# Compressed keys and values in a hybrid decoder block: the first product with the weights stationary

## The chip, the cores and the metric

The kernel runs on one core of a Trainium2 chip. The metric is the device time of one execution in microseconds (us). All arithmetic is float32; where a product runs on TensorE as float32r, each operand is split into a rounded high part and a low part (the rest), and the product is made of up to three products of parts.

## The reference

A decoder block over 256 tokens with 2048 features: one wide input projection, a gated short convolution beside sparse attention with 16 query heads and 4 key and value heads, a residual layer norm, an MLP and per-layer embeddings. What matters here is the compression of the keys and of the values, cut from the reference:

```python
def _compress(k, pe, w1, w2):
    B, T, Hk, Dh = k.shape                       # 1, 256, 4, 128
    n_cmp = (T - CMP_LEN) // CMP_STRIDE + 1      # 15 blocks of 32 tokens, 16 apart
    idx = jnp.arange(n_cmp)[:, None] * CMP_STRIDE + jnp.arange(CMP_LEN)[None, :]
    blocks = k[:, idx] + pe[None, None, :, None, :]
    blocks = jnp.moveaxis(blocks, 3, 2).reshape(B, n_cmp, Hk, CMP_LEN * Dh)
    return jax.nn.gelu(blocks @ w1) @ w2         # w1: 4096 x 256, w2: 256 x 128
```

Four heads with 15 blocks each are 60 rows; the first product has 4096 features to sum over, in 32 slices of 128, and 256 hidden features as its result.

## The kernel before

The weights stream from memory in pieces of 512 KB at most. A piece is loaded by SyncE's queue into one of four buffers (`raw`, L74), ScalarE writes its rounded high part (`whi`, L68, four buffers), VectorE the low part (`wlo`, L69, three buffers), and TensorE uses both. The big projections have two forms. `wstat` (L98, L104) takes 256 columns of the weights as stationary operand: per slice of 128 features two products of 512 moving columns (both parts of the tokens) and two of 256. `xstat` (L124, L125, L128) takes the tokens as stationary operand and moves 512 or 280 columns of weights.

The order of the work is written out by generators. `weave` runs a main generator and a side generator, with the side's steps spread evenly over the main's. Here the main one has 40 steps, four `wstat` of four steps each (keys of the two other branches) and three `xstat` of eight; the side one is `compress` for the keys and then for the values, 24 steps. The order of TensorE's instructions in the trace differs a little from that of the program: a product whose low part isn't ready yet stands behind later work.

`compress` first lays out the 60 blocks by position (`blk`, both parts, L263 to the split). Then, for each of the 32 positions `l`, it multiplies: the blocks' two parts, 120 columns side by side, are the stationary operand, and the 256 hidden features of the weights' high part (L273) and of their low part (L274) move. The result `ph` has the blocks on partitions, in one PSUM bank (tag `po`). ScalarE copies it out (L277), two transposes (L281) bring the features onto partitions in another bank (tag `tp`), and VectorE adds the two halves (L286, L287) and computes the gelu with ScalarE's tanh (L288 to L293). The second product follows a step later: for the keys L298 (float32, 60 moving columns), for the values L317 (float32, 64 stationary and 128 moving columns), both in the bank `po`.

Of the kernel before, what the change touches and what calls it, by code (L numbers as in the profile page):

```python
# [10 lines left out]
F32 = mybir.dt.float32  # L11
# [5 lines left out]
P = 128  # L17
# [8 lines left out]
HID = 2 * HD  # L26
# [6 lines left out]
GELU_C = 0.7978845608028654  # L33
# First distances of the log-spaced buckets 16, 17, ... (distances below 16 have one bucket each).
LOG_STARTS = (16, 23, 32, 46, 64, 91, 128, 182)

# Column offsets of w_in.
C_BG, C_CG, C_HX, C_Q = 0, D, 2 * D, 3 * D
# [7 lines left out]
def block_kernel(ctx: ExitStack, tc: tile.TileContext, x, p, w_in, conv_w, cmp_pe_k, cmp_w1_k, cmp_w2_k,  # L46
# [24 lines left out]
    def load_raw(src, nk, n):  # L71
        """A [nk*128, n] piece of a weight matrix, rows on partitions."""
        raw = wp.tile([P, nk, n], F32, tag="raw", name="raw", bufs=4)
        nc.sync.dma_start(raw, src.rearrange("(k p) n -> p k n", p=P))  # L74
        return raw

    def wchunk(src, nk, n):
        """The same as two float32r parts."""
        raw = load_raw(src, nk, n)
        hi = wp.tile([P, nk, n], F32R, tag="whi", name="whi", bufs=4)  # L80
        lo = wp.tile([P, nk, n], F32R, tag="wlo", name="wlo", bufs=3)
        split(raw, hi, lo)
        return hi, lo

    def wstat(src, c0, mov, evac, r0=0, nk=4, ahead=None):
        """256 columns of src as the stationary operand, both parts of mov side by side as the moving one.
        evac(f, A, B): features f*128 .. of the result are A + B, [feature, token] each."""
        ps = [ps_mm.tile([P, 2, T], F32, tag="mm", name="mm") for _ in range(2)]
        for k0 in range(0, KT, nk):
            hi, lo = wchunk(src[r0 + k0 * P:r0 + (k0 + nk) * P, c0:c0 + 256], nk, 256)  # L90
            for kk in range(nk):
                kt = k0 + kk
                if ahead is not None:
                    ahead(kt)

                def high():
                    for f in range(2):
                        nc.tensor.matmul(ps[f].rearrange("p a t -> p (a t)"), hi[:, kk, f * P:(f + 1) * P],  # L98
                                         mov[:, kt].rearrange("p a t -> p (a t)"), start=(kt == 0),
                                         stop=(kt == KT - 1), skip_group_check=True)  # L100

                def low():
                    for f in range(2):
                        nc.tensor.matmul(ps[f][:, 1, :], lo[:, kk, f * P:(f + 1) * P], mov[:, kt, 0, :],  # L104
                                         start=False, stop=False, skip_group_check=True)

                for part in ((high, low) if kt < KT - 1 else (low, high)):
                    part()
            yield
        for f in range(2):  # L110
            evac(f, ps[f][:, 0, :], ps[f][:, 1, :])

    def xstat(src, c0, n, sta, evac, r0=0, nkt=KT, ahead=None):
        """n columns of src as the moving operand, sta as the stationary one: evac(t, [token, n])."""
        ps = [ps_mm.tile([P, n], F32, tag="mm", name="mm") for _ in range(NT)]
# [26 lines left out]
    def weave(main, n_main, side, n_side):  # L142
        """Steps of side spread evenly over the steps of main."""
        done = 0
# [5 lines left out]

# [1 line left out]
    ident = const.tile([P, P], F32, name="ident")  # L152
    make_identity(nc, ident)
    NV = (3 + 2) * KT
    vecT = const.tile([P, NV], F32, name="vecT")  # conv taps, then ln1 gain and offset, features on partitions
    gate = const.tile([P, NT, 3 * NH], F32, name="gate")
# [9 lines left out]
    def transposed(nat, kt):  # L166
        """Columns kt*128 .. of two 128-token tiles, features on partitions."""
        pool, tag = turns[kt // 2 % len(turns)]
# [19 lines left out]

    # In these the two float32r parts are the dimension before the last, or before the branch in the keys.
    att = ctx.enter_context(ExitStack())  # L190
# [9 lines left out]
    with tc.tile_pool(name="front", bufs=1) as fp:  # L200
# [19 lines left out]

        # Taps, gains and offsets by feature; bias by distance, -127 up to 255.
        vecs = fp.tile([NV, P], F32, name="vecs")
# [21 lines left out]

# [1 line left out]
        nb = NKV * NCMP  # L246
        blk = big.tile([P, 2, CMP_LEN, 2, NKV * NCMP], F32R, tag="B", name="blk")

        def compress(i, pe, w1, w2):
# [16 lines left out]
            yield  # L266
            ph = ps_po.tile([2 * nb, HID], F32, tag="po", name="ph")
            for l4 in range(CMP_LEN // 4):
                hi, lo = wchunk(w1[0][l4 * 512:(l4 + 1) * 512, :], 4, HID)
                for k in range(4):  # L270
                    l = 4 * l4 + k
                    b = blk[:, i, l].rearrange("p a n -> p (a n)")
                    nc.tensor.matmul(ph, b, hi[:, k, :], start=(l == 0), stop=False)  # L273
                    nc.tensor.matmul(ph, b, lo[:, k, :], start=False, stop=(l == CMP_LEN - 1))  # L274
                yield
            hs = fp.tile([2 * nb, HID], F32, tag="hs", name="hs")
            nc.scalar.activation(hs, ph, AF.Copy)  # L277
            yield
            tp = ps_tp.tile([P, 2, 2, 64], F32, tag="tp", name="tp")
            for e in range(2):  # L280
                nc.tensor.transpose(tp[:, e].rearrange("p a n -> p (a n)")[:, :2 * nb],  # L281
                                    hs[:, e * P:(e + 1) * P], ident[:2 * nb, :2 * nb])
            both = tp.rearrange("p e a n -> p e (a n)")
            g0 = fp.tile([P, 2, nb], F32, tag="g0", name="g0")
# [19 lines left out]
            else:  # L304
                # A row of vrep for each of a group's four heads and 16 blocks, the last of which is zero.
                hx = ap.tile([P, 2, NKV, 4, 16], F32, tag="s1", name="hx")
# [15 lines left out]
        def v_window(lo_cols):  # L322
            # The window's values and the gates' logits are 560 columns side by side.
            def evac(t, ps):
# [7 lines left out]
        def keys(i, h):  # L332
# [5 lines left out]
        weave(chain(*proj), 40, chain(compress(0, cmp_pe_k, cmp_w1_k, cmp_w2_k),  # L338
                                      compress(1, cmp_pe_v, cmp_w1_v, cmp_w2_v)), 24)

# [1 line left out]
    o = big.tile([P, NH, T], F32, tag="O", name="o")  # L342
# [8 lines left out]
    def conv_block(cp, c):  # L351
        """Channels c*128 .. c*128 + 255."""
        cg = cp.tile([P, 2, T], F32, tag="cg", name="cg")
# [22 lines left out]

    # Products of two split operands: parts of the one and of the other.
    parts = ((0, 0), (1, 0), (0, 1))
# [4 lines left out]
    def attend(j, q):  # L383
        """Heads 4j .. 4j + 3, of key and value head j."""
        # bias[q, g, i] is at distance q + i - 127, so that key k of the first w keys is at i = w - 1 - k.
        bias = ap.tile([P, 4, T], F32, tag="bias", name="bias", bufs=1)
# [5 lines left out]
        nc.vector.tensor_copy(cb[:, 1, :, 0:15], back(bias, 224, (T, 4), (-16, 15)))  # L392
        # The compressed keys as columns (g, c) for head g, zero elsewhere.
        nc.vector.tensor_copy(back(kcp, 0, (4 * 64, 2), (64 + 16, 4), (1, 16)),
# [66 lines left out]
        def values(pair, pT):  # L461
            """Two heads' outputs, [feature, query tile, head, query]."""
            # Row (g, c) of the compressed values for head g, zero elsewhere.
            vm = ap.tile([64, 2, 2, HD], F32R, tag="vm", name="vm", bufs=1)
# [25 lines left out]
        for g in range(4):  # L490
# [3 lines left out]
            if g % 2 == 0:  # L494
                # Of each part and branch the blocks (keys 0, queries 0), (0, 1), (1, 1) of two heads.
                pT = ap.tile([P, 2, 2, 3, 2, P], F32R, tag="pT", name="pT", bufs=1)
# [18 lines left out]

# [1 line left out]
    post = ctx.enter_context(tc.tile_pool(name="post", bufs=2))  # L517
# [30 lines left out]

# [1 line left out]
    xres = big.tile([P, NT, D], F32, tag="O", name="xres")  # L550
# [31 lines left out]

# [1 line left out]
    x1 = big.tile([P, KT, 2, T], F32R, tag="X", name="x1")  # L584
# [51 lines left out]

# [1 line left out]
    stats2 = post.tile([P, NT, 4, 6], F32, tag="st", name="stats2", bufs=1)  # L638
# [48 lines left out]

    # The last columns with all their weights at hand, so that the first tokens are done early.
    wh = big.tile([P, KT, 512], F32R, tag="X", name="wh")
# [21 lines left out]
def _onehot():  # L711
    """Bucket of each distance -127 .. 255, a column each; the last row stands for what is masked."""
    e = np.zeros((NB + 1, 384), np.float32)
# [45 lines left out]
```

## Time and profile before

| | |
|---|---|
| median of 3 runs | 1865.37 us (1864.33 to 1865.76) |
| span of the profiled execution | 1864.0 us |
| TensorE matmul, busy | 1839.1 us (99%) |
| TensorE weight load, busy | 1577.8 us (85%) |
| VectorE, busy | 1157.9 us (62%) |
| ScalarE, busy | 879.3 us (47%) |

The profile gives the profiled execution by its span, from its first instruction to its last; the median of the runs is 1.37 us above it. Durations of matmuls overlap, since they are pipelined and their ends are modelled, so the distance from one start to the next says more of the pace than a duration does. PE stands for matmuls and PEld for weight loads of TensorE, DVE for VectorE, ACT for ScalarE, SP for SyncE.

### The profile page before, as it was taken

The page shows a single profiled execution, that of the slowest core. Times are in us where ns is not written, and L with a number is a line of the kernel's source. Part 1 is how long each engine was busy: PE and PEld are TensorE (multiplying, and loading weights), DVE is VectorE, ACT ScalarE, POOL GpSimd, SP SyncE. Part 2 cuts the span into 40 slices and gives each one's busy share as a digit, 9 for nine tenths or more (in the row PEclk, how much of TensorE's full clock was granted, in tenths as well). Part 3 has the DMA queues.
Part 4 walks back from the last instruction along what each step waited for, and adds up shares of the span by engine and source line. Part 5 has one row for each costly group of instructions (what it writes and reads, how often), then busy time and mean ns, then how long its engine had stood idle before and what let it go on. Part 6 is the DMA issues. An engine that isn't in the chain of part 4 may idle for free.

```text
span 1864.0 us, 25953 instructions
## 1 busy us (share of the span) xinstructions
PE 1839.1 (99%) x9921; PEld 1577.8 (85%) x9921; DVE 1157.9 (62%) x1668; ACT 879.3 (47%) x1269; POOL 43.2 (2%) x42
## 2 busy tenths in 40 slices
PE   8999999999999999999999899999999999999997
PEld 7889888888888888888888688888888888888886
DVE  6676776767677555565555865655565556556664
ACT  5555554545556444444443444443444344434541
POOL 1000000000000000000000500000000000000001
PEclk9999999999999999999999999999999999999998
DMA  8767565555555766666665466655665566556671
GB/s 249 231 201 240 171 170 164 164 169 170 160 165 171 220 188 187 192 192 183 191 236 193 169 204 192 191 191 188 196 187 191 193 189 190 192 192 192 193 243 72
DMA packets 295068, 352.98 MB, mean 189 GB/s; under 512 B 11125, under 2 KB 240853, under 8 KB 294176
## 3 DMA queue, kind: packets, MB, share of 16 engines
q1 hardware_dynamic: 291328, 342.27, 59.5%
q10 hardware_dynamic: 3232, 8.65, 1.3%
q8 instruction: 77, 1.26, 0.3%
q0 software_dynamic: 384, 0.41, 0.1%
q14 instruction: 47, 0.39, 0.1%
HBM read 349.17 MB, written 2.12 MB: 188 GB/s over the span
## 4 chain that ended last, share of the span: by engine, by line
PE 96%; DVE 2%; DMA 1%; issue 0%; ACT 0%; SPq 0%; POOLq 0%; POOL 0%; DVEq 0%
PE mm L98 42%; PE mm L104 21%; PE mm L125 9%; PE mm L124 9%; PE mm L128 9%; PE mm L705 1%; PE pss L436 1%; DVE x L69 1%; PE po L473 1%; DMA raw<-in_w_mlp_down_dram 1%; PE tp L458 1%; DVE wlo L69 0%; PE ph L274 0%; PE ph L273 0%; PE po L482 0%; PE po L477 0%
## 5 line engine op out<-in xcount | busy, mean ns | idle before, releaser
L69 DVE TENSOR_TENSOR wlo<-raw,whi 128x1024 fp32r<-128x1024 f32 (+2 forms) x648 | 781.6, 1209 | 596.7 <-PE mm L104 298.6
L68 ACT ACTIVATE whi<-raw 128x1024 fp32r<-128x1024 f32 (+2 forms) x648 | 676.8, 1046 | 683.3 <-PE mm L98 314.6
L98 PE MATMUL mm<-xT,whi 128*128 128x512 f32 x1792 | 562.7, 397 | 0.0
L104 PEld LDWEIGHTS mm<-xT,wlo 128*128 128x128 f32 x1792 | 328.6, 188 | 73.3 <-issue 0.2
L104 PE MATMUL mm<-xT,wlo 128*128 128x256 f32 x1792 | 349.0, 280 | 0.0
L98 PE MATMUL mm<-x,whi 128*128 128x512 f32 x1024 | 316.8, 395 | 0.0
L98 PEld LDWEIGHTS mm<-xT,whi 128*128 128x128 f32 x1792 | 279.3, 189 | 6.0 <-issue 0.6
L104 PEld LDWEIGHTS mm<-x,wlo 128*128 128x128 f32 x1024 | 187.9, 188 | 42.5
L104 PE MATMUL mm<-x,wlo 128*128 128x256 f32 x1024 | 196.7, 279 | 0.0
L125 PE MATMUL mm<-whi,h 128*128 128x512 f32 x480 | 186.8, 389 | 0.0
L124 PE MATMUL mm<-whi,h 128*128 128x512 f32 x480 | 186.7, 389 | 0.0
L98 PEld LDWEIGHTS mm<-x,whi 128*128 128x128 f32 x1024 | 158.4, 189 | 2.8
L128 PE MATMUL mm<-wlo,h 128*128 128x512 f32 x480 | 147.9, 389 | 0.6 <-DVE wlo L69 0.6
L128 PEld LDWEIGHTS mm<-wlo,h 128*128 128x128 f32 x480 | 90.0, 188 | 19.6 <-DVE wlo L69 1.0
L125 PEld LDWEIGHTS mm<-whi,h 128*128 128x128 f32 x480 | 90.1, 188 | 18.8
L124 PEld LDWEIGHTS mm<-whi,h 128*128 128x128 f32 x480 | 90.1, 188 | 18.7
L98 PE MATMUL mm<-aT,whi 128*128 128x512 f32 x256 | 80.4, 395 | 0.0
L98 PE MATMUL mm<-oT,whi 128*128 128x512 f32 x256 | 80.3, 395 | 0.0
L104 PEld LDWEIGHTS mm<-oT,wlo 128*128 128x128 f32 x256 | 47.0, 188 | 10.6
L104 PEld LDWEIGHTS mm<-aT,wlo 128*128 128x128 f32 x256 | 46.9, 188 | 10.5
L125 PE MATMUL mm<-whi,x 128*128 128x512 f32 x128 | 50.2, 404 | 2.8 <-DVE x L69 2.8
L125 PE MATMUL mm<-whi,mix 128*128 128x512 f32 x128 | 49.8, 389 | 0.0
(210 smaller groups left out, 1636.5 us busy)
## 6 DMA issues: line engine op xcount, KB each, us to landing
raw<-in_w_in_dram SPq DMA_DIRECT2D x228, 512.0 KB, 3.7
raw<-in_w_mlp_up_dram SPq DMA_DIRECT2D x128, 512.0 KB, 3.8
raw<-in_w_mlp_down_dram SPq DMA_DIRECT2D x128, 512.0 KB, 3.8
raw<-in_w_conv_out_dram SPq DMA_DIRECT2D x32, 512.0 KB, 3.4
raw<-in_w_attn_out_dram SPq DMA_DIRECT2D x32, 512.0 KB, 3.4
raw<-in_w_mix_out_dram SPq DMA_DIRECT2D x32, 512.0 KB, 4.0
raw<-in_w_ple_gate_dram SPq DMA_DIRECT2D x32, 512.0 KB, 4.1
raw<-in_w_in_dram SPq DMA_DIRECT2D x16, 280.0 KB, 3.4
```

The lines of the kernel that those rows point to most:

```text
L68: nc.scalar.activation(hi, src, AF.Copy)
L69: nc.vector.tensor_sub(lo, src, f32(hi))
L98: nc.tensor.matmul(ps[f].rearrange("p a t -> p (a t)"), hi[:, kk, f * P:(f + 1) * P], mov[:, kt].rearrange("p a t -> p (a t)"), start=(kt ...
L104: nc.tensor.matmul(ps[f][:, 1, :], lo[:, kk, f * P:(f + 1) * P], mov[:, kt, 0, :], start=False, stop=False, skip_group_check=True)
L124: nc.tensor.matmul(ps[t], sta[:, kt, 0, ts], hi[:, kk, :], start=(kt == 0), stop=False)
L125: nc.tensor.matmul(ps[t], sta[:, kt, 1, ts], hi[:, kk, :], start=False, stop=False)
L128: nc.tensor.matmul(ps[t], sta[:, kt, 0, ts], lo[:, kk, :], start=False, stop=(kt == nkt - 1))
L436: nc.tensor.matmul(ps, q[:, g, a, t * P:(t + 1) * P], kT[:, j, b, :, :w], start=(n == 0), stop=(n == 2))
L458: nc.tensor.transpose(tp[:, b, k, :], s[:, b, k * P:(k + 1) * P], ident)
L473: nc.tensor.matmul(po, vn[:, b, 0, a, vs], pT[:, c, b, 0:2], start=(n == 0 and b == 0), stop=False, skip_group_check=True)
L705: nc.tensor.matmul(ps, h[:, kt, a, ts], w[:, kt, :], start=(kt == 0 and n == 0), stop=(kt == KT - 1 and n == 2))
```

## The change

The first product of `compress` changes its form. For each position the weights' 128x128 pieces are now the stationary operand, two halves `e` of the hidden features with a high and a low part each. The blocks move: both parts (120 columns) over a high piece, the high part alone (60 columns) over a low piece, added to the columns of the blocks' low part. So there are four products a position in place of two, and the product of the two low parts is left out. The result `ph` has the features on partitions, so the copy by ScalarE and the two transposes go, with one step, and VectorE reads `ph` itself. Keys and values together have 22 side steps in place of 24. The other lines of the diff are comments, which are left out here.

```diff
-            ph = ps_po.tile([2 * nb, HID], F32, tag="po", name="ph")
+            ph = ps_po.tile([P, 2, 2 * nb], F32, tag="po", name="ph")
             for l4 in range(CMP_LEN // 4):
                 hi, lo = wchunk(w1[0][l4 * 512:(l4 + 1) * 512, :], 4, HID)
                 for k in range(4):
                     l = 4 * l4 + k
                     b = blk[:, i, l].rearrange("p a n -> p (a n)")
-                    nc.tensor.matmul(ph, b, hi[:, k, :], start=(l == 0), stop=False)
-                    nc.tensor.matmul(ph, b, lo[:, k, :], start=False, stop=(l == CMP_LEN - 1))
+                    for e in range(2):
+                        es = slice(e * P, (e + 1) * P)
+                        nc.tensor.matmul(ph[:, e, :], hi[:, k, es], b, start=(l == 0 and e == 0), stop=False,
+                                         skip_group_check=True)
+                        nc.tensor.matmul(ph[:, e, nb:], lo[:, k, es], b[:, :nb], start=False,
+                                         stop=(l == CMP_LEN - 1 and e == 1), skip_group_check=True)
                 yield
-            hs = fp.tile([2 * nb, HID], F32, tag="hs", name="hs")
-            nc.scalar.activation(hs, ph, AF.Copy)
-            yield
-            tp = ps_tp.tile([P, 2, 2, 64], F32, tag="tp", name="tp")
-            for e in range(2):
-                nc.tensor.transpose(tp[:, e].rearrange("p a n -> p (a n)")[:, :2 * nb],
-                                    hs[:, e * P:(e + 1) * P], ident[:2 * nb, :2 * nb])
-            both = tp.rearrange("p e a n -> p e (a n)")
+            both = ph
...
-                                      compress(1, cmp_pe_v, cmp_w1_v, cmp_w2_v)), 24)
+                                      compress(1, cmp_pe_v, cmp_w1_v, cmp_w2_v)), 22)
```

## Rows read from the trace of the kernel before

**Rows 1.** The page's busy shares: busy us, share of the span and instructions, TensorE's matmuls and weight loads.

```profile
PE 1839.1 (99%) x9921; PEld 1577.8 (85%) x9921; DVE 1157.9 (62%) x1668; ACT 879.3 (47%) x1269; POOL 43.2 (2%) x42
```

**Rows 2.** The page's chain of work that ended last, share of the span by engine.

```profile
PE 96%; DVE 2%; DMA 1%; issue 0%; ACT 0%; SPq 0%; POOLq 0%; POOL 0%; DVEq 0%
```

**Rows 3.** Busy time of each engine in the two windows that hold the compression: window and its length, then PE, PEld, DVE, ACT and POOL busy us with instructions, granted TensorE clock as a share of 2.4 GHz, DMA share, GB/s.

```profile
36.00:120.00 84.00, 84.00 (x492) 73.78 (x491) 55.55 (x68) 45.78 (x60) 0.00 (x0) 1.00 0.74 226
120.00:175.00 55.00, 53.86 (x359) 49.18 (x358) 38.63 (x53) 31.08 (x43) 0.74 (x1) 1.00 0.73 218
```

**Rows 4.** Matmuls of the compression grouped by line and shape, from 36 to 600 us: line, engine, operation, output and inputs, stationary operand (partitions * columns), moving operand (partitions x columns), count | busy us, mean ns of one | idle us before.

```profile
L273 PE MATMUL ph<-whi,blk 128*120 128x256 f32 x64 | 16.4, 283 | 0.6 <-DVE blk L69 0.6
L274 PE MATMUL ph<-wlo,blk 128*120 128x256 f32 x64 | 15.9, 282 | 0.0
L281 PE MATMUL tp<-ident,hs 120*128 120x120 f32 x4 | 0.7, 265 | 0.0
```

**Rows 5.** One step of the first product in the timeline (start us, duration us): its first matmul, its last, and the next operation's.

```profile
76.37 0.28 PE L273 MATMUL ph<-whi,blk 128*120 128x256 f32 x1
...
77.19 0.28 PE L274 MATMUL ph<-wlo,blk 128*120 128x256 f32 x1
...
77.30 0.62 PE L98 MATMUL mm<-xT,whi 128*128 128x512 f32 x2
```

**Rows 6.** Weight loads grouped by line and shape, from 36 to 600 us, columns as in rows 4. L399, L273 and L98 load float32r; L298 is a float32 product; L458 and L424 load for transposes.

```profile
L98 PEld LDWEIGHTS mm<-xT,whi 128*128 128x128 f32 x1246 | 194.3, 189 | 3.8
...
L458 PEld LDWEIGHTS tp<-ident,s 128*128 128x128 f32 x96 | 11.7, 140 | 1.6
...
L273 PEld LDWEIGHTS ph<-whi,blk 128*120 128x120 f32 x64 | 11.6, 181 | 1.3 <-issue 0.8 <-ACT whi L68 0.2
...
L399 PEld LDWEIGHTS pq<-q,kcp 128*64 128x64 f32 x48 | 5.9, 134 | 0.4
...
L424 PEld LDWEIGHTS tp<-ident,cs 128*64 128x64 f32 x8 | 0.9, 111 | 0.5
...
L298 PEld LDWEIGHTS pk<-g,w2s 128*128 128x128 f32 x4 | 0.6, 190 | 0.1
```

**Rows 7.** The second product of the keys (L298) between matmuls of 512 columns in the timeline; a row with x4 holds four instructions.

```profile
122.50 0.39 PE L124 MATMUL mm<-whi,xT 128*128 128x512 f32 x1
122.50 0.64 PEld L298 LDWEIGHTS pk<-g,w2s 128*128 128x128 f32 x4
...
122.72 0.55 PE L298 MATMUL pk<-g,w2s 128*128 128x60 f32 x4
123.06 0.19 PEld L125 LDWEIGHTS mm<-whi,xT 128*128 128x128 f32 x1
123.08 0.48 PE L125 MATMUL mm<-whi,xT 128*128 128x512 f32 x1
123.17 0.19 PEld L124 LDWEIGHTS mm<-whi,xT 128*128 128x128 f32 x1
...
123.40 0.39 PE L124 MATMUL mm<-whi,xT 128*128 128x512 f32 x1
```

**Rows 8.** TensorE's timeline, a matmul of 512 columns five slices (30 starts) before the first of rows 7.

```profile
115.69 0.39 PE L124 MATMUL mm<-whi,xT 128*128 128x512 f32 x1
```

**Rows 9.** TensorE's timeline, two matmuls of 280 columns six starts apart.

```profile
159.28 0.29 PE L124 MATMUL mm<-whi,xT 128*128 128x280 f32 x1
...
160.05 0.29 PE L124 MATMUL mm<-whi,xT 128*128 128x280 f32 x1
```

**Rows 10.** The transposes (L281) in the timeline, for the keys among matmuls of 512 columns and for the values among matmuls of 280.

```profile
112.29 0.63 PE L128 MATMUL mm<-wlo,xT 128*128 128x512 f32 x2
...
112.75 0.37 PE L281 MATMUL tp<-ident,hs 120*128 120x120 f32 x2
...
113.20 0.39 PE L125 MATMUL mm<-whi,xT 128*128 128x512 f32 x1
...
162.87 0.42 PE L128 MATMUL mm<-wlo,xT 128*128 128x280 f32 x2
...
163.13 0.37 PE L281 MATMUL tp<-ident,hs 120*128 120x120 f32 x2
...
163.48 0.29 PE L125 MATMUL mm<-whi,xT 128*128 128x280 f32 x1
```

**Rows 11.** Matmuls of the timeline ahead of which TensorE sat idle, with the idle us and what ended them in brackets.

```profile
134.11 0.35 PE L273 MATMUL ph<-whi,blk 128*120 128x256 f32 x1 [0.56 <-DVE blk L69]
...
145.87 0.40 PE L124 MATMUL mm<-whi,xT 128*128 128x280 f32 x1 [0.40 <-ACT whi L68]
...
153.10 0.40 PE L124 MATMUL mm<-whi,xT 128*128 128x280 f32 x1 [0.18 <-ACT whi L68]
```

**Rows 12.** The first and the last of VectorE's operations on the keys' sums and gelu in the timeline.

```profile
114.49 0.28 DVE L286 COPY g<-tp 128x120 f32<-128x120 f32 x1
...
117.94 0.28 DVE L293 TENSOR_TENSOR g<-g,g 128x120 f32<-128x120 f32 x1
```

**Rows 13.** The second product of the values in the timeline, 16 float32 matmuls in one row.

```profile
174.12 1.96 PE L317 MATMUL pv<-w2s,hx 128*64 128x128 f32 x16
```

## Prediction

> **What bounds the kernel now.** I read first the page's busy shares and the chain that ended last. The reader should see TensorE's matmul row at 99% of the span and a chain that is TensorE's for 96% [rows 1, 2]; VectorE and ScalarE feed it and mostly wait. Then the windows around the change: compression lies between 36 and 175 us, where matmuls fill all 84.00 us of the first window and 53.86 of the 55 us of the second, at a granted clock of 1.00, the 2.4 GHz level [rows 3]. So a nanosecond added to or taken from TensorE's stream there is one of the run, nearly one for one. A busy share doesn't say what sets the pace of the stream, though: weight loads run on a row of their own beside the matmuls, and the slower of the two decides. Hence the rest is read from start to start in the timeline, not from durations, which overlap.
>
> **Part 1: the first product, before.** There are 64 products with the high part and 64 with the low one, each 256 moving columns over a stationary operand of 120 columns [rows 4]. A step of eight starts at 76.37, and the next operation's matmul at 77.30: 0.93 us for eight, 0.116 us each [rows 5]. All 128: 14.9 us.
>
> **Part 2: the first product, after.** Each of the 64 weight slices now needs four products: two of 120 moving columns (high) and two of 60 (low), each with its own stationary operand of 128x128. So 256 loads stand where 128 did, with 23,040 moving columns (64 x 360) in place of 32,768. Two candidates for the pace:
>
> By columns. Starts in the streams of 512 columns lie 0.227 us apart (30 starts from 115.69 to 122.50) [rows 7, 8] and in those of 280 columns 0.128 us (six starts from 159.28 to 160.05) [rows 9]: 0.43 ns a column and some 0.01 us each. That makes 0.06 us for 120 columns and 0.035 for 60.
>
> By loads. Durations of float32r loads grow with the stationary columns: 134 ns at 64, 181 at 120, 189 at 128 [rows 6]. The slope is 0.84 ns a column between the first two, so a load of 128 columns would occupy the path for some 0.107 us, the rest being latency. The nearest row for a short moving operand is the second product of the keys, float32 with 60 moving columns on 128x128 weights: four pairs of load and matmul. The 512-column matmul ahead starts at 122.50, the second one behind at 123.40. Without the four, these two starts would take 2 x 0.227 = 0.454 us; the four cost 0.446, or 0.112 us each. Their loads show the same: two behind them start at 123.06 and 123.17, 0.11 apart [rows 7]. Sixty columns there were covered entirely by a load. That operand is float32 and the change's is float32r, but the durations agree (190 and 189 ns) [rows 6], so I take 0.112.
>
> 256 x 0.112 = 28.7 us, against 14.9: **+13.8 us**. Lower end, by the slope: 256 x 0.107 = 27.4, +12.5. Upper end, if each short product takes what one of 256 columns takes: 256 x 0.116 = 29.7, +14.8. The four products of a slice have four different operands, so no load can be shared, and a long matmul ahead hides only the first load of a step.
>
> **Part 3: what goes.** Two transposes for each of keys and values [rows 4]. At the first place TensorE goes from 112.29 to 113.20 in 0.91 us, three ordinary starts (0.68) and the pair: 0.23. At the second, from 162.87 to 163.48 in 0.61 us, three starts of 0.128 (0.38) and the pair: 0.23 [rows 10]. Together **-0.45 us**. The ScalarE copy ahead of them goes too; its cover is that ScalarE is busy for only 45.78 of 84.00 us and 31.08 of 55 [rows 3]. I give nothing for it.
>
> **Part 4: what moves.** The side work has 22 steps instead of 24 over the same 40 main steps. Worked out from the loop, the gelu chain stays behind main steps 17 and 37, the second products behind 19 and 39, and the set-up of values behind 21; only the eight weight steps of each part spread by up to one main step. VectorE now reads the sums from the bank of the first product. The next writer of that bank is the second product, which already waits for the end of that chain, so no new wait is added. The chain went from 114.49 to 118.22, and its product came at 122.50 to 122.72 [rows 7, 12]: 4.3 us of cover; without it, TensorE would wait for the chain's 3.7 us, twice.
>
> Three TensorE waits lie in this stretch: 0.56 us on the blocks' low part at 134.11, and 0.40 and 0.18 us on ScalarE's split weights at 145.87 and 153.10 [rows 11]. The first has its cause in the set-up, whose place stays. The other two come from weights that arrive faster than they can be split; when the products between them take almost twice as long, ScalarE has more time for each piece. I take both as gone: **-0.58 us**; ends -1.14 (all three go) and 0. A different spread may move the order of instructions a little later on, which no row prices; I allow 2 us each way.
>
> **The sum.** +13.8 - 0.45 - 0.58 = +12.8 us. The profiled execution's span is 1864.0 us, the runs' median 1865.37, so 1.4 us lie around the span or between executions. 1864.0 + 12.8 + 1.4 = **1878.2 us**, +0.7%. Bounds: 12.5 - 0.45 - 1.14 = +10.9 (1876.3) and 14.8 - 0.45 = +14.4 (1879.8); with 2 us for the order, 1874.3 to 1881.8.
>
> **Rivals.**
>
> B, columns decide (not slower). If a load of 128 float32r columns can hide under 60 moving columns, the products take 128 x (0.060 + 0.035) = 12.2 us, -2.7; with -0.45 and -0.58 that is -3.7, **1861.7 us**. For it: in transposes, loads of float32 grow only from 111 ns at 64 columns to 140 at 128 [rows 6], 0.45 ns a column, so the path can be faster. Against it: the change's loads are not of that form, and float32r loads keep the steeper slope up to 128 columns. It decides once a load occupies less than about 0.06 us; at that price 256 loads just cost what the products did before.
>
> On this the Trainium skill (TensorE: Matmul & The Clock Gate, Weight-path perf modes) says that weights load fast when there are exactly 128 of them and the input type is not FP32. If float32r counted as not FP32, the old 120-column loads would miss that and the new ones get it, and the sum would be B's. The trace doesn't bear it out: the 128-column loads, at 189 ns, aren't quicker than the 120-column ones, at 181 [rows 6].
>
> C, short float32r products run in two passes. The float32 products of 60 columns stand as four records for two calls, two loads each [rows 7]; no row before shows a float32r product under 256 columns. Doubled, 512 x 0.112 = 57.3 us, +42.4 - 0.45 - 0.58: **1906.8 us**. Against it: every float32r product has one record now, 64 for 64 [rows 4]. One pass at half the rate would change nothing: the float32 products of 128 columns start 16 times in 1.96 us [rows 13], about 0.11 each, which a load covers.
>
> D, the chain's cover goes. If the second products are scheduled right behind their gelu chain, TensorE waits up to 3.7 us twice: **1885.6 us**. The two main steps between speak against it.
>
> **Chances.** The forecast 0.80 (nearly all of it inside its bounds), B 0.07, C 0.06, D 0.07. The range reaches from the forecast's low bound to part of D: 1874 to 1884, some 0.8. This kernel's measurement tells 0.2%, 3.7 us, from no change. B lies on that edge and is halved between faster and same; all other cases are slower: faster 0.03, same 0.04, slower 0.93.
>
> **What would show it.** Part 2: 256 loads under the first product's line, starts about 0.112 us apart whether 60 or 120 columns move, and a step of sixteen of some 1.8 us; B would show starts alternating between 0.06 and 0.035. C: 512 records. Part 3: no transposes between product and gelu. Part 4: no wait ahead of the second products, and the waits near 145 and 153 us smaller. The sum is wrong if the granted clock falls under 1.00 in this stretch: then the products ahead and behind take longer too.

## The result and the profile after

| | before | after |
|---|---|---|
| median | 1864.33 us (1864.21 to 1865.76, 5 runs) | 1875.69 us (1874.45 to 1877.57, 5 runs) |
| ratio of the runs | | 1.0056, 95% interval 1.0046 to 1.0067 |
| span of the profiled execution | 1864.0 us | 1873.5 us |

The changed kernel is slower by 0.56%: some 10.4 us by the ratio (8.6 to 12.5 by its interval), 11.4 us by the two medians and 9.5 us by the two profiled spans. Forecast were 12.8 us and a time between 1874 and 1884.

The page's busy shares after, to be read beside [rows 1]:

```profile
PE 1849.1 (99%) x10045; PEld 1590.6 (85%) x10045; DVE 1156.9 (62%) x1668; ACT 879.2 (47%) x1267; POOL 40.9 (2%) x42
```

Shares say nothing here: 99% before and after. The 124 additional matmuls are 128 more products less four transposes. The two windows of [rows 3]:

```profile
36.00:120.00 84.00, 84.00 (x526) 74.78 (x525) 57.81 (x72) 44.60 (x58) 0.00 (x0) 1.00 0.70 209
120.00:175.00 55.00, 55.00 (x383) 51.69 (x382) 30.91 (x42) 25.84 (x35) 0.74 (x1) 1.00 0.68 199
```

The second was busy for 53.86 of 55 us and has no idle time now; the granted clock is still 1.00. The loads and matmuls of the first product (duration ns minimum/median/maximum, first and last start us):

```profile
L276 PEld LDWEIGHTS ph<-blk,whi x128: 187/192/192, 63.5 to 170.7; 128*128 128x128 f32 x128
L276 PE MATMUL ph<-blk,whi x128: 217/302/305, 63.6 to 170.8; 128*128 128x120 f32 x128
L278 PEld LDWEIGHTS ph<-blk,wlo x128: 187/192/192, 63.6 to 170.8; 128*128 128x128 f32 x128
L278 PE MATMUL ph<-blk,wlo x128: 189/246/248, 63.7 to 170.9; 128*128 128x60 f32 x128
```

There are 256 records for 256 products, one pass each. One step of sixteen in the timeline, the answer to [rows 5]:

```profile
78.39 0.22 PE L276 MATMUL ph<-blk,whi 128*128 128x120 f32 x1
...
78.53 0.30 PE L276 MATMUL ph<-blk,whi 128*128 128x120 f32 x1
...
78.66 0.25 PE L278 MATMUL ph<-blk,wlo 128*128 128x60 f32 x1
...
78.75 0.30 PE L276 MATMUL ph<-blk,whi 128*128 128x120 f32 x1
...
79.86 0.30 PE L276 MATMUL ph<-blk,whi 128*128 128x120 f32 x1
...
80.00 0.25 PE L278 MATMUL ph<-blk,wlo 128*128 128x60 f32 x1
...
80.09 0.71 PE L98 MATMUL mm<-xT,whi 128*128 128x512 f32 x2
```

Starts of one line lie 0.22 us apart: six pairs from 78.53 to 79.86 are 1.33 us, 0.222 a pair. A product of 60 columns starts 0.13 us after its neighbour and the next one 0.09 later, 0.111 on the mean. The loads of the same step start evenly, 0.11 us apart, whatever moves:

```profile
79.72 0.19 PEld L278 LDWEIGHTS ph<-blk,wlo 128*128 128x128 f32 x1
79.84 0.19 PEld L276 LDWEIGHTS ph<-blk,whi 128*128 128x128 f32 x1
79.95 0.19 PEld L278 LDWEIGHTS ph<-blk,wlo 128*128 128x128 f32 x1
80.06 0.30 PEld L98 LDWEIGHTS mm<-xT,whi 128*128 128x128 f32 x2
```

The two long matmuls behind the step span 0.71 us instead of the usual 0.63: the first one's load began only at 80.06, 0.03 us ahead of its matmul instead of some 0.11, and could not hide behind a product of 60 columns.

Where the time came in is seen from work far behind the change: attention's transposes, before and then after (first and last start at the end of the times):

```profile
L458 PE MATMUL tp<-ident,s x96: 270/272/274, 224.5 to 583.4; 128*128 128x128 f32 x96
```

```profile
L456 PE MATMUL tp<-ident,s x96: 270/272/274, 234.8 to 593.7; 128*128 128x128 f32 x96
```

Both ends moved by 10.3 us, so all of it arose ahead of 224 us and none was added by attention. The profiled executions then differ by another -0.8 us around the layer norms and at the end. That part, and the wait for the first data at the start, differ by up to 1.8 us among the profiled executions of all the kernels here, which are alike in these places, so the stretch from 44 to 200 us is compared from here on.

**One measure for all kernels.** For each group of the first product's matmuls in the timeline: from the last other matmul ahead of it to the second one behind it, less what these two distances take elsewhere in the stretch without a group between (the median for the same lines and columns). The sum over all groups is what the first product costs TensorE's stream, with the loads it leaves unhidden and the waits in it.

| kernel | products | cost of the first product, us | median ratio to before (95%) |
|---|---|---|---|
| before | 128 | 17.67 | |
| after | 256 | 28.60 | 1.0056 (1.0046 to 1.0067) |
| a240 | 256 | 28.74 | 1.0054 (1.0039 to 1.0069) |
| a64 | 256 | 17.73 | 0.9996 (0.9987 to 1.0006) |
| b_dbl | 256 | 30.88 | 1.0067 (1.0052 to 1.0082) |
| b_even | 128 | 15.62 | 0.9984 (0.9975 to 0.9993) |
| b_lay | 128 | 16.73 | 0.9992 (0.9982 to 1.0001) |
| a_late | 256 | 29.29 | 1.0058 (1.0042 to 1.0074) |
| a_even | 256 | 28.56 | 1.0053 (1.0035 to 1.0071) |

From before to after, +10.93 us for the product and -0.45 for the transposes make +10.5; the starts moved by 10.3, so 0.2 us are not accounted for.

### The profile page after: what moved, and what is told of

Same layout as the page of the kernel before. It is cut to its first block, busy times and chain, and to the rows that moved or that the text cites. A ratio compares the mean times of both kernels' runs of the same rounds, so it can differ in the third digit from the quotient of the medians.

```text
span 1873.5 us, 26186 instructions
## 1 busy us (share of the span) xinstructions
PE 1849.1 (99%) x10045; PEld 1590.6 (85%) x10045; DVE 1156.9 (62%) x1668; ACT 879.2 (47%) x1267; POOL 40.9 (2%) x42
## 4 chain that ended last, share of the span: by engine, by line
PE 95%; DMA 2%; DVE 2%; issue 0%; ACT 0%; SPq 0%; POOLq 0%; POOL 0%; DVEq 0%; ACTq 0%
PE mm L98 41%; PE mm L104 21%; PE mm L128 9%; PE mm L124 9%; PE mm L125 9%; PE mm L703 1%; DMA raw<-in_w_mlp_down_dram 1%; PE pss L434 1%; PE ph L276 1%; DVE wlo L69 1%; PE po L471 1%; DMA raw<-in_w_ple_gate_dram 1%; PE tp L456 1%; DVE x L69 1%; PE ph L278 1%
## 5 line engine op out<-in xcount | busy, mean ns | idle before, releaser
L98 PE MATMUL mm<-xT,whi 128*128 128x512 f32 x1792 | 563.5, 397 | 0.0
L98 PE MATMUL mm<-x,whi 128*128 128x512 f32 x1024 | 316.8, 395 | 0.0
L98 PEld LDWEIGHTS mm<-xT,whi 128*128 128x128 f32 x1792 | 279.3, 189 | 6.2 <-issue 0.8
L98 PEld LDWEIGHTS mm<-x,whi 128*128 128x128 f32 x1024 | 158.5, 189 | 2.8
L98 PE MATMUL mm<-aT,whi 128*128 128x512 f32 x256 | 80.3, 395 | 0.0
L98 PE MATMUL mm<-oT,whi 128*128 128x512 f32 x256 | 80.3, 395 | 0.0
L104 PEld LDWEIGHTS mm<-aT,wlo 128*128 128x128 f32 x256 | 46.9, 188 | 10.5
```

## The experiments

**Theories.** L: the loads of 128 stationary columns set the pace, 0.112 us each. Against it, K: the moving columns do; and F: a short float32r product has a fixed price, whatever is loaded. The forecast's sum was 2.5 us too high (12.8 against the 10.3 by which the starts moved), though its product term fits, so a second question is where that came from. V: the product before held 2.6 us of waits (17.67 less 128 x 0.118), which longer steps dissolve. O: the waits went by the other spread of steps. How the wait on the values' blocks went was split off when b_dbl was in: H, by a bank that came free; P, by VectorE's gained time.

**a240: more than twice the columns, the same loads.**

```diff
-            ph = ps_po.tile([P, 2, 2 * nb], F32, tag="po", name="ph")
+            ph = ps_po.tile([P, 2, 2, 2 * nb], F32, tag="po", name="ph")
-                    b = blk[:, i, l].rearrange("p a n -> p (a n)")
+                    b = blk[:, i, l].rearrange("p a n -> p (a n)")[:, None, :].to_broadcast([P, 2, 2 * nb])
-                        nc.tensor.matmul(ph[:, e, :], hi[:, k, es], b, ...
-                        nc.tensor.matmul(ph[:, e, nb:], lo[:, k, es], b[:, :nb], ...
+                        nc.tensor.matmul(ph[:, e], hi[:, k, es], b, ...
+                        nc.tensor.matmul(ph[:, e], lo[:, k, es], b, ...
-            both = ph
+            both = ph[:, :, 0, :]
```

> The changed kernel, with all four products of a position over 240 moving columns (the 120 columns of the blocks twice); only the first 120 columns of the result are read. 256 loads as before, 61,440 moving columns instead of 23,040. If weight loads of 128 columns set the pace (theory L), a product of 240 columns needs 0.43 ns x 240 + 0.01 = 0.113 us, the same as its load: a step of sixteen stays at 1.8 us and the time within 0.5 us of the changed kernel's (+10 us over before). If the moving columns set it (rival K), 38,400 more of them at 0.43 ns add 16.5 us.

The low parts' product is kept here, since the low weights meet all columns. Its step in TensorE's timeline:

```profile
79.38 0.27 PE L276 MATMUL ph<-blk,whi 128*128 128x240 f32 x1
...
81.06 0.28 PE L278 MATMUL ph<-blk,wlo 128*128 128x240 f32 x1
81.17 0.40 PE L98 MATMUL mm<-xT,whi 128*128 128x512 f32 x1
```

Sixteen products in 1.79 us, 0.112 each, now evenly. The cost is 28.74 us against 28.60: 38,400 further columns cost 0.14 us. K falls.

**a64: the same columns, loads half as wide.**

```diff
-                        es = slice(e * P, (e + 1) * P)
+                        es = slice(e * P, e * P + 64)
-                        nc.tensor.matmul(ph[:, e, :], ...
+                        nc.tensor.matmul(ph[:64, e, :], ...
-                        nc.tensor.matmul(ph[:, e, nb:], ...
+                        nc.tensor.matmul(ph[:64, e, nb:], ...
-            nc.vector.tensor_copy(g0, both[:, :, :nb])
-            nc.vector.tensor_add(g0, g0, both[:, :, nb:2 * nb])
+            nc.vector.memset(g0, 0.0)
+            nc.vector.tensor_copy(g0[:64], both[:64, :, :nb])
+            nc.vector.tensor_add(g0[:64], g0[:64], both[:64, :, nb:2 * nb])
```

> The changed kernel with only 64 of each 128 weight columns as stationary operand: the same 256 products with the same moving columns, loads half as wide; half of the hidden features are left out (zeros in their place). Theory L: a load of 64 columns occupies about 0.054 us, the products take 0.06 (120 columns) and 0.054 us, 14.6 us in all instead of 28.6, so 14.0 us less than the changed kernel; of the 2.6 us of TensorE waits that the first product had in the kernel before, some come back, as a step is as short as it was there: 11.4 to 14.0 us less, about 1862 to 1864.5 us. Rival F, a fixed price of some 0.11 us for every short float32r product whatever is loaded: no change against the changed kernel, about 1874.5 us.

The loads' line, and one step in TensorE's timeline:

```profile
L276 PEld LDWEIGHTS ph<-blk,whi x128: 133/138/140, 64.2 to 160.7; 128*64 128x64 f32 x128
```

```profile
77.49 0.22 PE L276 MATMUL ph<-blk,whi 128*64 128x120 f32 x1
...
77.57 0.25 PE L276 MATMUL ph<-blk,whi 128*64 128x120 f32 x1
...
78.27 0.25 PE L276 MATMUL ph<-blk,whi 128*64 128x120 f32 x1
78.36 0.20 PE L278 MATMUL ph<-blk,wlo 128*64 128x60 f32 x1
78.39 0.47 PE L98 MATMUL mm<-xT,whi 128*128 128x512 f32 x1
```

A step starts and ends within 0.90 us instead of 1.70, with the same sixteen products. The cost falls by 10.9 us and the time to that of before. F falls, though the fall lies short of the 11.4 to 14.0 us expected. Inside a step the price was as expected: six pairs from 77.57 to 78.27 are 0.70 us, 0.058 a product against the 0.057 of 0.06 and 0.054 in turn. What the 14.6 us left out are the loads of 128 columns behind each of the 28 groups of products, some 0.05 us each that no short product hides: a step of sixteen cost 0.98 us with it and a product by itself 0.11. By the groups without waits all products cost 16.4 us, 1.8 more than expected, and the remaining 1.3 us are waits, 1.1 of them at one place (158.73). The change had none: waits are back once steps are short, with the changed kernel's own spread of steps, which speaks against O. One thing a64 doesn't part: with the load it also halves the rows of the result that a product writes.

The Trainium skill (TensorE: Matmul & The Clock Gate, LDWEIGHTS) gives a load's time in ns as its columns divided by 1.2, which makes 107 ns for 128 and 53 for 64. The traces bear that out as a floor, with 0.112 and 0.058 us a product in a stream, the latter with 120 and 60 moving columns in turn. The fast load of 128 columns that the Trainium skill describes (the same page, Weight-path perf modes) is not seen: the 128-column loads took 192 ns, the 64-column ones 138.

**b_dbl: longer steps with the old form.**

```diff
+                    for n in range(2):
-                    nc.tensor.matmul(ph, b, hi[:, k, :], start=(l == 0), stop=False)
-                    nc.tensor.matmul(ph, b, lo[:, k, :], start=False, stop=(l == CMP_LEN - 1))
+                        nc.tensor.matmul(ph, b, hi[:, k, :], start=(l == 0 and n == 0), stop=False)
+                        nc.tensor.matmul(ph, b, lo[:, k, :], start=False, stop=(l == CMP_LEN - 1 and n == 1))
-            nc.scalar.activation(hs, ph, AF.Copy)
+            nc.scalar.activation(hs, ph, AF.Copy, scale=0.5)
```

> The kernel before with each of its 128 products issued twice into the same sum and the copy scaled by 0.5: the result is the same, and a step takes as long as the changed kernel's or longer. The 128 further products of 256 columns cost 128 x 0.117 = 15.0 us. Theory V, the 2.6 us of waits in the first product came from split weights and blocks that were late for short steps: they go, and the time is 12.4 us over before. Rival O, they went in the changed kernel by its other spread of steps: they stay here, 15.0 us over before.

The ratio is 12.5 us over before, but its interval, 9.7 to 15.3 us, holds the figures of both theories; the span is 12.5 us over too. The trace decides: the cost grew by 13.2 us where 128 further products at 0.118 are 15.1, so 1.9 us of waits went and not 2.6. One wait stayed, with 0.85 us between these starts instead of 0.13 (idle us and what ended them in brackets):

```profile
141.31 0.29 PE L125 MATMUL mm<-whi,xT 128*128 128x280 f32 x1
142.16 0.35 PE L274 MATMUL ph<-whi,blk 128*120 128x256 f32 x1 [0.56 <-DVE blk L69]
```

So V holds for the waits on split weights and not for the one on the values' blocks, though VectorE had all the time that longer steps give.

**b_even: the old form with its steps spread by time.** `weave_by` is `weave` with the time of each main step in place of its count; `layout` is the part of `compress` up to the split of the blocks.

```diff
+                if i == 0 and l4 == 3:
+                    layout(1, cmp_pe_v)
+                    yield
...
-        weave(chain(*proj), 40, chain(...), 24)
+        weave_by(chain(*proj), [2.8] * 16 + [2.72] * 8 + [1.54] * 16, chain(...), 24)
```

> The kernel before with its form of the first product and its transposes, but the side steps spread over the time of the main steps instead of over their number (the sixteen steps of 280 columns count 1.54, the others 2.8 and 2.72), and the layout of the values' blocks moved into the middle of the keys' steps. Theory V: late pieces no longer meet dense steps, most of the 2.6 us of waits go, 1.5 to 2.6 us under before, 1862 to 1863 us; at most some of it comes back as a wait for the gelu chain, which now has one main step of cover in places. Rival O: waits stay where they are, no change.

The cost fell by 2.05 us and the time by 0.16% (0.07 to 0.25%). TensorE's only wait on another engine listed between 36 and 200 us:

```profile
PE ph L287 <- ACT whi L68: 0.2, 1, 0.2
```

The waits were there to be taken without any change of the product's form. This version is faster than both kernels. Since it changes the spread of the steps itself, it says nothing against O; b_dbl and a64 do.

**b_lay: only the values' layout moved.** The first hunk of b_even with `weave` by number.

> The kernel before with one move: the layout of the values' blocks (transpose of the positions, four adds, the split) stands in the middle of the keys' steps, ahead of the keys' two transposes; the side steps stay spread by number, 24 on 40. Theory H, in the changed kernel the wait of 0.7 us ahead of the values' first product went because the removed transposes no longer hold the one bank of the tag tp, so that the values' layout runs some 65 us earlier: here the layout runs early as well and that wait goes, -0.7 us, while the later waits for split weights (1.9 us in all) stay, so about 1863.5 to 1864 us against 1864.5 to 1865.5 of before. Rival P, that wait went because the slower products gave VectorE time: it stays here, no change. The trace tells these apart, the runs hardly.

VectorE's copies of the keys' and of the values' positions, the second one 77.6 us earlier than before:

```profile
L265 DVE COPY peT<-tp x2: 184/184/185, 25.6 to 48.1; 128x32 f32<-128x32 f32 x2
```

The last low-part matmuls of the projection and the first of the values' products in TensorE's timeline:

```profile
132.59 0.62 PE L128 MATMUL mm<-wlo,xT 128*128 128x512 f32 x2
133.05 0.28 PE L287 MATMUL ph<-whi,blk 128*120 128x256 f32 x1
```

No wait. The cost fell by 0.94 us, the 0.8 of that wait and a little, and the later waits stayed. By the runs alone it can't be told from before.

**a_late: the changed kernel with the bank taken away.**

```diff
-            tp = ps_tp.tile([P, CMP_LEN], F32, tag="tp", name="tp")
+            pool, tag = ((ps_tp, "tp"), (ps_po, "po"))[i]
+            tp = pool.tile([P, CMP_LEN], F32, tag=tag, name="tp")
```

> The changed kernel with the transpose of the values' positions written into the bank of the keys' products (tag po) instead of the free one (tag tp), so that the values' layout can start only after the keys' second product, as in the kernel before. Theory H: the layout runs at some 127 us instead of 47 and TensorE waits some 0.7 us ahead of the values' first product again; +0.7 us on the changed kernel. Rival P: the slower products leave VectorE enough time, no wait, no change.

The cost is 29.29 us against 28.60: +0.69. VectorE's copy of the values' positions, and TensorE ahead of the values' first product:

```profile
133.56 0.18 DVE L258 COPY peT<-tp 128x32 f32<-128x32 f32 x1
```

```profile
141.16 0.29 PE L125 MATMUL mm<-whi,xT 128*128 128x280 f32 x1
141.92 0.32 PE L277 MATMUL ph<-blk,whi 128*128 128x120 f32 x1 [0.47 <-DVE blk L69]
```

The wait is back with the slow products in place: P falls. In the changed kernel the same copy and the split's end stood here in VectorE's timeline, and TensorE passed the place without a pause:

```profile
47.81 0.18 DVE L257 COPY peT<-tp 128x32 f32<-128x32 f32 x1
...
63.62 2.16 DVE L69 TENSOR_TENSOR blk<-O,blk 128x1920 fp32r<-128x1920 f32 x1 [0.87 <-ACT blk L68]
```

```profile
133.36 0.62 PE L128 MATMUL mm<-wlo,xT 128*128 128x512 f32 x2
...
133.81 0.22 PE L276 MATMUL ph<-blk,whi 128*128 128x120 f32 x1
```

Before, the copy came at 125.67, since the keys' two transposes used the one bank of that tag in between:

```profile
125.67 0.18 DVE L257 COPY peT<-tp 128x32 f32<-128x32 f32 x1
```

**a_even: the changed kernel spread by time.** Both hunks of b_even, with 22 steps.

> The changed kernel with the side steps spread over the time of the main steps and the values' layout placed early, the edit that took 2 us from the kernel before. Theory V: the changed kernel has no waits left in its first product, so nothing is to be gained: within 0.5 us of the changed kernel, 10 us over before. If the spread gains by something other than those waits, it gains 2 us here too.

28.56 against 28.60 us, a ratio of 1.0053: no waits left, nothing gained, as V has it.

## Why the prediction was right, and what it mis-sized

**Part 1, the old product:** 0.116 us each was read from one step; the mean without waits is 0.118, so 15.1 us instead of 14.9. Small.

**Part 2, the new product: right.** 28.7 us forecast, 28.60 measured. The price came from four float32 products of the same shape, with the distance across the group rather than the durations, and held for float32r. a240 and a64 show that it is the price of the load: 38,400 further columns cost 0.14 us, and with half the stationary columns a product took 0.058 us instead of 0.111.

**Part 3, the transposes: right**, 0.45 us in the same measure. That the copy's removal is worth nothing was argued and not tested alone.

**Part 4, the waits: mis-sized**, -0.58 us forecast, with -1.14 as the far end, where -2.6 came; this is 2.0 of the 2.5 us (Part 1 has 0.2, Part 2 0.1, and 0.2 are not accounted for). It failed in two places. First, "the first has its cause in the set-up, whose place stays": its place among the steps stayed, but the removed transposes freed a bank, and the set-up ran 78 us earlier. a_late and b_lay show that from both sides. Second, idle time was taken for the loss. The profile lists 0.40 and 0.18 us at 145.87 and 153.10 [rows 11]; these starts of before say more:

```profile
145.18 0.28 PE L273 MATMUL ph<-whi,blk 128*120 128x256 f32 x1
...
152.54 0.38 PE L273 MATMUL ph<-whi,blk 128*120 128x256 f32 x1
...
153.59 0.29 PE L125 MATMUL mm<-whi,xT 128*128 128x280 f32 x1
...
153.80 0.38 PE L274 MATMUL ph<-wlo,blk 128*120 128x256 f32 x1
...
157.31 0.28 PE L273 MATMUL ph<-whi,blk 128*120 128x256 f32 x1
157.56 0.40 PE L124 MATMUL mm<-whi,xT 128*128 128x280 f32 x1
```

From 145.18 to 145.87 are 0.69 us where 0.12 would do, a loss of 0.57 against 0.40 listed, and 0.1 more for the load behind it that could not be hidden. Two further losses, ahead of 153.80 and 157.56, have no idle time listed at all: the modelled end of the matmul ahead covers them. By the measure above the five places hold 2.6 us, 0.8 of them ahead of 134.11 and 1.8 in the other four.

**The rivals:** B (columns) and C (two passes) did not come: a step takes 1.8 us, and there are 256 records. D did not come either: no wait of TensorE stands ahead of the second products, the keys' chain starting at 114.33 and their product at 125.17:

```profile
114.33 0.28 DVE L284 COPY g<-ph 128x120 f32<-128x120 f32 x1 [0.42 <-PE ph L278]
```

```profile
124.72 0.61 PE L128 MATMUL mm<-wlo,xT 128*128 128x512 f32 x2
125.17 0.55 PE L296 MATMUL pk<-g,w2s 128*128 128x60 f32 x4
```

The order of instructions behind the change, for which 2 us were allowed, cost nothing: the distance stays 10.3 us through all of attention.

**What was luck.** The measured 1875.69 us lies under the 1876.3 that the terms of the sum gave as their low bound. It is inside the stated range only by the 2 us allowed for the order of instructions, and what took them up was mostly the mis-sized waits.

## What to carry to other kernels

When a change swaps the stationary and the moving operand, count loads as well as columns: the slower of the two sets the pace, and its price is found in whatever product of that shape the trace already holds, by the distance across it. Waits are sized from start to start and not from idle time, with the load that is exposed behind each. When a step goes, look at what else used its buffer: what was queued behind that buffer moves too, however far.

## What was not expected of the hardware

Moving 240 columns over a freshly loaded 128x128 operand cost no more than moving 120 and 60 in turn (0.112 us a product in both cases), so such a load leaves room for some 240 columns that cost nothing. A product by itself between long matmuls cost some 0.11 us in the changed kernel, with loads of 128 columns, and as much in a64, with loads of 64: what nothing hides there is the load of the long matmul behind it.
